# A group norm's root by Ln and Exp and decay differences by Relu on ScalarE, in a state-space layer that TensorE fills

## The chip, the core and the metric

The kernel runs on one core of a Trainium2 chip. A core has TensorE (PE in the profile: matmuls, with PEld for the weight loads), VectorE (DVE), ScalarE (ACT), GpSimd (POOL) and SyncE (SP), each with its own queue of instructions that runs in order; semaphores hold an instruction until what it needs from another engine or a transfer is there. The metric is the device time of one execution in microseconds (us).

## The reference, cut to what matters

Two layers, each a token mixer and a gated FFN, for 512 tokens of width 1024 in float32. Layer 0 mixes by a short convolution, layer 1 by a Mamba-2 state-space layer with 8 groups of 4 heads. Only parts of the second layer are touched:

```python
    cs = jnp.cumsum((dt * a).reshape(bsz, nc, l, g, r), axis=2)
    seg = cs[:, :, :, None] - cs[:, :, None]
    decay = jnp.exp(jnp.where(causal, seg, -jnp.inf)).astype(dtype)
    cb = jnp.einsum('bclgn,bcsgn->bclsg', cm, bm)
    y_diag = jnp.einsum('bclsgr,bcsgrp->bclgrp', cb[..., None] * decay, xdt)
...
    y = y.reshape(bsz, s, M_D_INNER) * jax.nn.silu(z)
    y = rms_normalize(y.reshape(bsz, s, g, M_D_INNER // g)).reshape(bsz, s, M_D_INNER) * norm_g
    return y @ w_out
...
        y = swiglu_ffn(h, f_w_in[i], f_w_out[i])
        x = x + gate * rmsnorm(y, norm_g[i, 3])
```

`rms_normalize` multiplies by `1 / sqrt(mean(x * x) + 1e-6)`.

## The kernel before

Every float32 matrix product is made of three matmuls: an operand is split into a high part (a cast on ScalarE, `act.copy`) and a low part (the rest, a subtraction on VectorE), and high x high, high x low and low x high are summed. Weights come in through the buffer `wst`, their two parts stand in tiles named `whl` or `whlo`, four buffers in a ring.

**The state-space layer** works its eight groups in turn. In all that the code calls `with tc.manual_schedule(...)`, the order in which instructions are written is the order on each engine. While group `cur` is evaluated, the projections of the next one (`nxt`) run on TensorE: four blocks of 24 matmuls for x (two), B and C, two for the gate z. Each of the four goes through `conv4` (L1360): a first step on ScalarE (`act.activation` with Identity, L1363), three on VectorE (L1366), a Silu on ScalarE (L1368). The work of `cur`:

- `prev.root()` and `prev.norm()` finish the group before: `ssg` holds the sums of squares in PSUM, ScalarE takes the root (L1551), VectorE the reciprocal over 128x512 (L1555), and two operations scale the group's outputs `yg` (L1558).
- `e_sub` (L1478): tile `csb` holds, in each of four 512 wide rows, the running sums of one head's decay; from each 128 wide piece a column of `cs_tok` is subtracted and the result clipped at zero from above. Sixteen instructions a group. `e_exp` (L1484): Exp over it, two instructions. `e_mul` (L1489): times the masked products of B and C.
- `step_a`: transposes of x and B and the products of B and C on TensorE, five operations on VectorE (L1433 to L1447), one eviction on ScalarE (`btok`, L1441).
- `states`: matmuls `st` (L1462), then `prev`, the state at the start of each chunk: a copy on ScalarE (L1465) and four small operations on VectorE (L1467, L1469).
- `step_cc`: matmuls `yo` (L1501, they read `prev`) and `yd` (L1512, they read `csb`), then four operations each on VectorE (L1517 to L1520) and the squares on ScalarE. `split_sq` and `sums` split these and sum them over partitions by a matmul (L1547), which gives the next `root` its `ssg`.

The steps of a group on VectorE stand in this order: the scaling of the group before, conv step of x0, a low weight part, `step_a`, `e_mul`, conv step of x1, a low weight part, `prev`, conv step of B, a low weight part, the operations on `yo` and `yd`, conv step of C, two low weight parts, the low part of the squares `sqs` and one more low weight part. Groups 1 to 6 are alike; group 0 is written out by hand ahead of the loop, and in group 7 there is no next group: in the place of its projections stand the first matmuls of the output projection (L381; `y_act`, L1568 and L1569, splits their operands `ys`).

**The layer's end.** `BOUNDARY` is a table of steps written by hand; it finishes the output projection, takes the post norm (`rt1`, L449, a Sqrt; then `x`, L456), the next pre norm (`xs`, L475, squares; `rt3`, L485; `xn`, L493, scaling) and transposes the result (`tr`, L502).

ScalarE's functions come in tables. Before an activation whose function the loaded table lacks, the built program has an ACT_TABLE_LOAD.

**The last FFN's second product** runs as 40 parts (`products`), each with its weights (`w_prep(n)`, L1980 and L1981) and its activations (`a_prep(n)`, L1993 and L1994) split some parts ahead. Four PSUM results, A to D, are collected in two token halves. After part n, `behind(n)` holds what becomes possible: squares for the norm (L2209), a product with the row of gates and norm weights `gg` (`gated`, L2219), sums of the results (L2246, which empties result A after part 33, before part 34 starts it anew). `got["11", t]` is one quarter of the result, in a tile c.

Of the kernel before, what the change touches and what calls it, by code (L numbers as in the profile page):

```python
# [10 lines left out]
AF = mybir.ActivationFunctionType  # L11
ALU = mybir.AluOpType
# [19 lines left out]
MUL, ADD, SUB = ALU.mult, ALU.add, ALU.subtract  # L32
# [6 lines left out]
def trunk_kernel(  # L39
# [9 lines left out]
    act, dve, pe, pool = nc.scalar, nc.vector, nc.tensor, nc.gpsimd  # L49
# [16 lines left out]
    def t2(name):  # L66
        return tmp.tile([P, T], F32, tag="t2", name=name, bufs=4)
# [10 lines left out]
    eps_t = consts.tile([P, 1], F32, name="eps")  # L78
# [501 lines left out]
    with ExitStack() as ph:  # L580
# [549 lines left out]
        def behind(q):  # L1130

            for t in range(2):
                if q == at["s", per - 1]:
                    held[0, t] = t2("c11")
                    act.copy(held[0, t], bank["A", t])
                elif q == at["s", 4 * per - 1]:
                    held[1, t] = t2("c12")
                    act.copy(held[1, t], bank["D", t])
                elif q == at["s", 5 * per - 1]:
                    dve.tensor_tensor(held[1, t], held[1, t], bank["A", t], SUB)  # L1140
                elif q == at["s", 6 * per - 1]:
                    held[1, 2 + t] = c22[:, t, :]
                    act.activation(c22[:, t, :], bank["A", t], AF.Copy, scale=-1.0)
            for p in range(n_s):
                if q == 5 + p // 2:
                    add_(b_("b22", p), b_("b12", p))
                if q == 12 + p:
                    add_(b_("b21", p), b_("b22", p))
                if q == 9 + p:
                    dve.tensor_tensor(b_("b11", p), b_("b22", p), b_("b11", p), SUB)  # L1150

        with tc.manual_schedule(engines={PE_ENGINE, mybir.EngineType.SP, mybir.EngineType.Activation,
# [74 lines left out]
            for q, item in enumerate(seq):  # L1227
                if item[0] == "s":
                    product(item)
                else:  # L1230
                    w = w_of[item]
                    plain_tiles(item[1], [(item[2] + kk, w, kk) for kk in range(2)], item[3])
                behind(q)
                if q in (0, 5):
                    list(rows_g[q // 5])
# [38 lines left out]
    with ExitStack() as ph:  # L1274
# [9 lines left out]
        cs_tok = consts.tile([P, NH, NCH], F32, name="cs_tok")  # L1284
# [89 lines left out]
        class Group:  # L1374
# [96 lines left out]
            def e_sub(self, q):  # L1471

                e = self.e[:, 2 * q:2 * q + 2]
                for hh in range(2):
                    for cc in range(NCH):
                        sl = slice(cc * P, (cc + 1) * P)
                        hd = 4 * self.g + 2 * q + hh
                        dve.tensor_scalar(e[:, hh, sl], e[:, hh, sl], cs_tok[:, hd, cc:cc + 1], 0.0,  # L1478
                                          SUB, ALU.min)

            def e_exp(self, q):

                e = self.e[:, 2 * q:2 * q + 2]
                act.activation(e, e, AF.Exp)  # L1484

            def e_mul(self, q):

# [60 lines left out]

            def root(self):
                self.rg = t2("rg")  # L1550
                act.activation(self.rg, self.ssg, AF.Sqrt, bias=eps_t, scale=1.0 / 256)  # L1551

            def norm(self):
                g = self.g
                dve.reciprocal(self.rg, self.rg)  # L1555
                for q in range(2):
                    y = ygs[2 * g + q]
                    dve.scalar_tensor_tensor(y, y, mng[:, 2 * g + q:2 * g + q + 1], self.rg, MUL, MUL)  # L1558
# [209 lines left out]
    with ExitStack() as ph:  # L1768
# [249 lines left out]
        with tc.manual_schedule(engines={PE_ENGINE, mybir.EngineType.SP, mybir.EngineType.Activation,  # L2018
# [5 lines left out]
            def t3(p):  # L2024
                i = unit_of[p]
                q = units[i].index(p)
                dve.tensor_tensor(b_(i, "b11", q), b_(i, "b22", q), b_(i, "b11", q), SUB)

            def t2_(i):
                add_(b_(i, "b22"), b_(i, "b12"))  # L2030

            def t4(i):
                add_(b_(i, "b21"), b_(i, "b22"))
# [172 lines left out]
            got = {}  # L2206

            def square(t, part, src):
                act.activation(spare["junk"], src, AF.Square, accum_out=st[t]["s2"][:, part:part + 1])  # L2209

            def mean(t):
                dve.tensor_scalar(st[t]["b1"], st[t]["s2"][:, 0:1], 1.0 / D, EPS, MUL, ADD)
# [5 lines left out]
            def gated(src, hf, dst):  # L2218
                dve.tensor_mul(dst, src, gg[hf])  # L2219
                return dst  # L2220

            def x_new(t, hf, yg, parts=(FULL,), puts=(dma,)):
                for c, put in zip(parts, puts):
                    cx = slice(hf * T + c.start, hf * T + c.stop)
                    dve.scalar_tensor_tensor(xt[t][:, cx], yg[:, c], st[t]["s1"], xt[t][:, cx], MUL, ADD)
                    put(out[0, t * P:(t + 1) * P, cx], xt[t][:, cx])

            def behind(n):

                for t in range(2):  # L2230
                    if n == 5:
                        got["11", t] = t2("c11")
                        act.copy(got["11", t], bank["A"][t])
                    elif n == 10:
                        dve.tensor_add(got["11", t], got["11", t], bank["B"][t])
                    elif n == 16:
                        got["12", t] = t2("c12")
                        act.copy(got["12", t], bank["C"][t])
                    elif n == 21:
                        dve.tensor_add(got["12", t], got["12", t], bank["D"][t])  # L2240
                        got["22", t] = spare[f"c22_{t}"]
                        act.copy(got["22", t], bank["D"][t])
                    elif n == 27:
                        dve.tensor_tensor(got["12", t], got["12", t], bank["A"][t], SUB)
                    elif n == 33:
                        dve.tensor_tensor(got["22", t], got["22", t], bank["A"][t], SUB)  # L2246
                    elif n in (29, 30):
                        if t == n - 29:
                            square(t, 0, got["11", t])
                            square(t, 1, got["12", t])  # L2250
                            mean(t)
                    elif n == 31:
                        gated(got["11", t], 0, got["11", t])
                    elif n == 34:
                        root(t)
                    elif n == 35:
                        square(2 + t, 0, got["22", t])
                        mean(2 + t)
                        gated(got["12", t], 1, got["12", t])
                        x_new(t, 0, got["11", t])  # L2260
                    elif n == 36:
                        gated(got["22", t], 1, got["22", t])
                        x_new(t, 1, got["12", t])
                for i, u in enumerate(units):
                    if n == 8 + u[-1] // 2:
                        t2_(i)
                    if n == 19 + i:
                        t4(i)
                for p in {26: (), 27: (), 28: (NP - 2,), 29: (NP - 1,)}.get(n, (n - 17,)):
                    if 0 <= p < NP:  # L2270
                        t3(turns[5][p])

            for n in range(NT - 3):
                if n not in (27, 33):
                    products([n])
                if n in (26, 32):
                    behind(n)
                    products([n + 1])
                    behind(n + 1)
                elif n < 34 and n not in (27, 33):  # L2280
                    behind(n)
                if n == 26:
                    for hf in range(2):
                        dma(gg[hf], gate_d[3, 4 * hf:4 * hf + 4].rearrange("j p -> (j p)").partition_broadcast(P))
                if n + 4 < NT:
                    w_prep(n + 4)
                if n + 3 < NT:
                    a_prep(n + 3)
                if n >= 34:
                    behind(n)  # L2290
            products(range(NT - 3, NT))
            for t in range(2):
                square(2 + t, 1, bank["A"][t])
                yg = gated(bank["A"][t], 0, t2("yg"))
                root(2 + t)
                if t == 0:
                    x_new(2, 0, yg)
                    x_new(2, 1, got["22", 0])
                else:
                    x_new(3, 1, got["22", 1])  # L2300
                    x_new(3, 0, yg, HALVES, (dma_s, dma))
# [29 lines left out]
```

## Time and profile before

| | us |
|---|---|
| median of three runs | 1328.46 (1328.2 to 1328.67) |
| profiled execution, its time | 1328.93 |
| profiled execution, its span | 1327.1 |
| a steady group of the state-space layer | 40.0 |
| TensorE busy | 1313.8 |
| VectorE busy | 1028.0 |
| ScalarE busy | 641.5 |

The span goes from the first to the last instruction, and the execution's own time holds a little more around it. The granted clock of TensorE was 0.999 of full speed on average. The profile gives a source line (L1551) for each instruction, its start and length, and in brackets how long its engine stood idle before it and what ended that. Instructions of one engine overlap a little, so that starts may follow each other more closely than the lengths say.

### The profile page before, as it was taken

How to read it: one execution, taken by the hardware profiler on the slowest of the kernel's cores; microseconds unless marked ns; L12 is line 12 of the kernel's file. 1: busy time of each engine (PE TensorE's matmuls, PEld its weight loads, DVE VectorE, ACT ScalarE, POOL GpSimd, SP SyncE). 2: the span in 40 equal slices, each digit the busy share in tenths (PEclk: the TensorE clock that was granted, in tenths of full speed). 3: DMA queues.
4: the chain of work that ended last, by engine and by line, in shares of the span. 5: the costliest groups of instructions: out<-in, count | busy, mean ns of one | idle time of the engine just before them, and what ended most of it. 6: DMA issues, size and time to landing. Idle time of an engine off the chain costs nothing.

```text
span 1327.1 us, 19226 instructions
## 1 busy us (share of the span) xinstructions
PE 1313.8 (99%) x7437; PEld 1134.4 (85%) x7437; DVE 1028.0 (77%) x1654; ACT 641.5 (48%) x1042; POOL 85.9 (6%) x106
## 2 busy tenths in 40 slices
PE   8999999999999999999999999999999999999997
PEld 7788889888888888898888888888789999998886
DVE  5588866788776686769998989888678777766897
ACT  5322357222222465665554555554574555544665
POOL 0000000000000140000000000000000111101320
PEclk9999999999999999999999999999999999999999
DMA  9757760688885692414534243413252788878961
GB/s 312 230 191 226 247 228 1 214 267 259 286 292 195 178 180 65 130 34 147 159 111 134 74 143 112 143 64 127 85 154 53 190 216 209 200 194 287 177 119 64
DMA packets 203456, 222.21 MB, mean 167 GB/s; under 512 B 8788, under 2 KB 148964, under 8 KB 202340
## 3 DMA queue, kind: packets, MB, share of 16 engines
q1 hardware_dynamic: 186496, 184.74, 44.7%
q0 software_dynamic: 12720, 23.34, 10.2%
q10 hardware_dynamic: 4148, 12.90, 3.0%
q8 instruction: 58, 0.95, 0.3%
q14 instruction: 34, 0.28, 0.1%
HBM read 195.37 MB, written 2.24 MB: 149 GB/s over the span
## 4 chain that ended last, share of the span: by engine, by line
PE 93%; DMA 2%; SPq 2%; DVE 1%; ACT 1%; issue 1%; DVEq 0%; ACTq 0%
PE ip L279 15%; PE ip L281 14%; PE ip L280 14%; PE y L381 8%; PE sA L1920 7%; PE cA L2015 4%; PE cA L1127 3%; PE sC L1920 3%; PE li L279 3%; PE li L281 3%; PE li L280 3%; PE sB L1920 2%; PE li L767 1%; PE yd L1512 1%; PE cC L2015 1%; PE cD L2015 1%
## 5 line engine op out<-in xcount | busy, mean ns | idle before, releaser
L279 PE MATMUL ip<-h,whl 128*128 128x512 f32 x840 | 331.6, 395 | 0.2 <-DVE cv L874 0.2
L281 PE MATMUL ip<-h,whl 128*128 128x512 f32 x840 | 327.6, 390 | 0.0
L280 PE MATMUL ip<-h,whl 128*128 128x512 f32 x840 | 327.4, 390 | 0.0
L279 PEld LDWEIGHTS ip<-h,whl 128*128 128x128 f32 x840 | 157.8, 188 | 33.7 <-issue 1.8
L281 PEld LDWEIGHTS ip<-h,whl 128*128 128x128 f32 x840 | 157.7, 188 | 33.2
L280 PEld LDWEIGHTS ip<-h,whl 128*128 128x128 f32 x840 | 157.9, 188 | 31.7
L225 DVE TENSOR_TENSOR whl<-wst,whl 128x1024 fp32r<-128x1024 f32 x99 | 120.4, 1221 | 41.6 <-ACT whl L224 41.5
L224 ACT CAST whl<-wst 128x1024 fp32r<-128x1024 f32 x99 | 102.3, 1042 | 61.2 <-DMA wst<-in_f_w_in_dram 49.9
L127 DVE SCALAR_TENSOR_TENSOR ada_acc<-ada_st,csil,ada_acc 128x512 f32<-128x512 f32 x140 | 105.0, 750 | 21.5 <-DMA ada_st<-in_ada_w_dram 18.1
L381 PE MATMUL y<-whlo,ys 128*128 128x512 f32 x384 | 89.4, 392 | 0.0
L381 PEld LDWEIGHTS y<-whlo,ys 128*128 128x128 f32 x384 | 71.8, 188 | 15.8 <-issue 0.7
L279 PE MATMUL li<-h,whl 128*128 128x256 f32 x288 | 83.4, 290 | 0.0
L281 PE MATMUL li<-h,whl 128*128 128x256 f32 x288 | 81.7, 284 | 0.0
L280 PE MATMUL li<-h,whl 128*128 128x256 f32 x288 | 81.6, 283 | 0.0
L1920 PE MATMUL sA<-tq,whl 128*128 128x256 f32 x576 | 74.6, 284 | 0.3 <-DVE g L1946 0.3
L1920 PEld LDWEIGHTS sA<-tq,whl 128*128 128x128 f32 x576 | 71.6, 192 | 0.6 <-DVE g L1946 0.5
L1366 DVE SCALAR_TENSOR_TENSOR cu<-ip,cols,cu 128x511 f32<-128x511 f32 (+2 forms) x84 | 62.8, 747 | 4.0 <-ACT cu L1363 1.4
L2015 PE MATMUL cA<-whlo,ao 128*128 128x512 f32 x264 | 61.0, 391 | 1.2 <-ACT whlo L1980 1.0
L2015 PEld LDWEIGHTS cA<-whlo,ao 128*128 128x128 f32 x264 | 49.3, 188 | 12.3 <-ACT whlo L1980 2.0
L1876 DVE TENSOR_TENSOR whl<-wsu,whl 128x1024 fp32r<-128x1024 f32 x33 | 40.4, 1223 | 23.4 <-ACT whl L1875 23.4
L279 PEld LDWEIGHTS li<-h,whl 128*128 128x128 f32 x288 | 55.3, 192 | 0.0
L280 PEld LDWEIGHTS li<-h,whl 128*128 128x128 f32 x288 | 55.3, 192 | 0.0
(371 smaller groups left out, 2319.5 us busy)
## 6 DMA issues: line engine op xcount, KB each, us to landing
ada_st<-in_ada_w_dram SPq DMA_DIRECT2D x96, 512.0 KB, 5.9
wst<-in_f_w_in_dram SPq DMA_DIRECT2D x26, 1024.0 KB, 7.2
wst<-in_m_w_in_dram SPq DMA_DIRECT2D x14, 1024.0 KB, 5.4
wst<-in_m_w_in_dram SPq DMA_DIRECT2D x20, 512.0 KB, 6.0
wst<-in_a_w_in_dram SPq DMA_DIRECT2D x9, 1024.0 KB, 6.8
wsu<-in_f_w_in_dram SPq DMA_DIRECT2D x17, 512.0 KB, 5.5
csb<-cs_d ACTq DMA_DIRECT2D x8, 1024.0 KB, 6.5
sg<-in_f_w_in_dram SPq DMA_DIRECT2D x32, 256.0 KB, 3.4
```

The lines of the kernel that those rows point to most:

```text
L127: dve.scalar_tensor_tensor(acc, w, csil[:, k:k + 1], acc, MUL, ADD)
L224: later.append((lambda sw=sw, w=w: act.copy(w[:, 0, :nk, :], sw), lambda sw=sw, w=w: dve.tensor_tensor(w[:, 1, :nk, :], sw, w[:, 0, :nk, : ...
L225: lambda sw=sw, w=w: dve.tensor_tensor(w[:, 1, :nk, :], sw, w[:, 0, :nk, :].bitcast(F32), SUB)))
L279: pe.matmul(dst, w_at(w, 0, kk), a[:, 0, sl], start=start, stop=False)
L280: pe.matmul(dst, w_at(w, 0, kk), a[:, 1, sl], start=False, stop=False)
L281: pe.matmul(dst, w_at(w, 1, kk), a[:, 0, sl], start=False, stop=stop)
L381: pe.matmul(pst, a[:, al, tk], wt[:, wl, kk, :], start=k == 0 and i == 0, stop=k == K - 1 and i == 2, skip_group_check=bool(held))
L1127: pe.matmul(bank[r, sub], a[:, al, q, tk], w[:, wl, q, :], start=first and k == 0, stop=False, skip_group_check=True)
L1366: dve.scalar_tensor_tensor(u[:, sft:], pst[:, :T - sft], w[3 - sft], u[:, sft:], MUL, ADD)
L1876: dve.tensor_tensor(dst[:, 1], src, dst[:, 0].bitcast(F32), SUB)
L1920: pe.matmul(dst, w[:, wl, k0 + k, :], moving(q, k, al), skip_group_check=True, start=q in ("P1", "P5", "P2") and k == 0 and i == 0, stop=k ...
L2015: pe.matmul(bank[r][sub], a[:, al, q, tk], w[:, hl, q, :], start=first and k == 0, stop=last and k == 2, skip_group_check=True)
```

## The change

Three edits. `root` takes Ln and then Exp with the scale -0.5, which gives the reciprocal root at once, and `norm` loses its reciprocal on VectorE. `e_sub` becomes a Relu on ScalarE, of the column less the piece, and `e_exp` takes the negative of it; VectorE loses sixteen instructions in each group, ScalarE gains as many. In the last FFN `behind` makes the two products of `got["11", t]` with the gates after part 30 and not after part 31.

```diff
-                        dve.tensor_scalar(e[:, hh, sl], e[:, hh, sl], cs_tok[:, hd, cc:cc + 1], 0.0,
-                                          SUB, ALU.min)
+                        act.activation(e[:, hh, sl], e[:, hh, sl], AF.Relu, bias=cs_tok[:, hd, cc:cc + 1],
+                                       scale=-1.0)
...
-                act.activation(e, e, AF.Exp)
+                act.activation(e, e, AF.Exp, scale=-1.0)
...
-                act.activation(self.rg, self.ssg, AF.Sqrt, bias=eps_t, scale=1.0 / 256)
+                act.activation(self.rg, self.ssg, AF.Ln, bias=eps_t, scale=1.0 / 256)
+                act.activation(self.rg, self.rg, AF.Exp, scale=-0.5)
...
-                dve.reciprocal(self.rg, self.rg)
...
                             mean(t)
-                    elif n == 31:
-                        gated(got["11", t], 0, got["11", t])
+                        if n == 30:
+                            gated(got["11", t], 0, got["11", t])
```

On ScalarE, at the start of each of the groups 1 to 6, with the norm's root (`rg`), the weight cast (`whl`), the decays (`csb`) and the first convolution step (`cu`):

```order
 L1551 ACT_TABLE_LOAD
 L1551 ACTIVATE rg<-ssg,eps 128x512
-L224 CAST whl<-wst 128x1024
-L1484 ACT_TABLE_LOAD
+L1552 ACT_TABLE_LOAD
+L1552 ACTIVATE rg<-rg 128x512
+L1478 ACTIVATE csb<-csb,cs_tok 128x128 x16
+L224 CAST whl<-wst 128x1024
 L1484 ACTIVATE csb<-csb 128x1024 x2
 L1363 ACTIVATE cu<-ip,cols_92,cols_93 128x512
```

The norm's Exp and sixteen Relu now stand ahead of the convolution's first step; the second table load moved from the decays' Exp to the norm's.

On ScalarE at the layer's end, where the post norm takes its first Sqrt (`ss`, the sums of squares):

```order
 L206 CAST whl_8223<-wst 128x512
 L433 ACTIVATE xn,ss<-y_7963 128x512
+L449 ACT_TABLE_LOAD
 L449 ACTIVATE ss<-ss 128x1
 L433 ACTIVATE xn,ss<-y_7603 128x512
```

One table load is new there; one more is new at the last group's norm, where Exp follows Ln.

On VectorE in the last FFN, parts 29 to 31 (`whlo` and `ao`: low parts of weights and activations; `c_11179` and `c_11181`: the two halves of `got["11", t]`; `ss`: the norm's first sum):

```order
 L1981 TENSOR_TENSOR whlo<-w2h_10998,whlo 128x512
 L1994 TENSOR_TENSOR ao<-raw,ao 128x512
+L2219 TENSOR_TENSOR c_11179<-c_11179,w2h_10992 128x512
 L2212 TENSOR_SCALAR ss<-ss 128x1
+L2219 TENSOR_TENSOR c_11181<-c_11181,w2h_10992 128x512
 L1981 TENSOR_TENSOR whlo<-w2t_10818,whlo 128x1024
 L1994 TENSOR_TENSOR ao<-raw,ao 128x256
-L2219 TENSOR_TENSOR c_11179<-c_11179,w2h_10992 128x512
-L2219 TENSOR_TENSOR c_11181<-c_11181,w2h_10992 128x512
 L1981 TENSOR_TENSOR whlo<-w2t_10913,whlo 128x1024
```

The two products move ahead of two low parts. TensorE's order is the same in both kernels.

## The prediction

> **What bounds the kernel now.** I read the page first, then the busy time of each engine over one group of the state-space layer, then TensorE's waits.
>
> ```profile
> span 1327.1 us, 19226 instructions
> PE 1313.8 (99%) x7437; PEld 1134.4 (85%) x7437; DVE 1028.0 (77%) x1654; ACT 641.5 (48%) x1042; POOL 85.9 (6%) x106
> 696.36:736.37 40.01, 40.01 (x217) 33.74 (x216) 35.71 (x58) 21.21 (x27) 1.30 (x1) 1.00 0.39 119
> PE cA L2015 <- ACT whlo L1980: 1.0, 1, 1.0
> PE cA L2015 <- DVE c L2244: 0.2, 1, 0.2
> ```
>
> TensorE (PE) is busy for 1313.8 of 1327.1 us. In a group of the state-space layer (third row: PE, weight loads, DVE, ACT) it is busy for all 40.01 us, VectorE for 35.71, ScalarE for 21.21. Nobody makes TensorE wait in that stage, so relieving VectorE can't shorten it. The question is what ScalarE's new work delays, and whether the slack in front of TensorE covers that.
>
> **The steady groups (1 to 6).** ScalarE at the start of such a group, then VectorE behind it, then TensorE's use of the result (the timeline: start, length):
>
> ```profile
> 726.77 1.28 ACT L1551 ACT_TABLE_LOAD   x1 [1.10 <-issue]
> 728.06 0.69 ACT L1551 ACTIVATE rg<-ssg,eps 128x512 f32<-128x512 f32 x1
> ...
> 729.71 1.28 ACT L1484 ACT_TABLE_LOAD   x1
> 731.00 2.01 ACT L1484 ACTIVATE csb<-csb 128x1024 f32<-128x1024 f32 x2
> 732.91 0.76 ACT L1363 ACTIVATE cu<-ip,cols,cols 128x512 f32<-128x512 f32 x1
> ...
> 728.78 3.35 DVE L1555 RECIPROCAL rg<-rg 128x512 f32<-128x512 f32 x1 [1.81 <-ACT rg L1551]
> 733.71 2.32 DVE L1366 SCALAR_TENSOR_TENSOR cu<-ip,cols,cu 128x511 f32<-128x511 f32 x3
> ...
> 747.06 0.42 DVE L1469 TENSOR_TENSOR prev<-prev,st 128x256 f32<-128x256 f32 x1
> ...
> 750.54 1.50 PE L1501 MATMUL yo<-ct,prev 128*128 128x128 f32 x12
> ```
>
> The convolution's first step on ScalarE (L1363) ends at 733.67, and VectorE's part (L1366) starts 0.04 us later. From there VectorE works without a gap, through the low weight parts, step_a, e_mul and the second convolution, to the last `prev` at 747.48 (747.06 + 0.42), 13.77 us on. The first `yo` product that reads it is the third of the first half, some 0.45 us after 750.54 (twelve records in 1.50 us, two for each product): 750.98. The cover is 3.5 us, 3.45 with the 0.04 of a signal.
>
> Ahead of that L1363 ScalarE gets an Exp over 128x512 and sixteen Relu over 128x128. The two table loads (Ln for Sqrt, Exp for Exp) stay two; the second only stands before the norm's Exp now. Ln over the same input is taken at Sqrt's 0.69. The trace has no Relu of this shape with a bias from a column; the nearest rows:
>
> ```profile
> 600.53 0.31 ACT L1335 ACTIVATE dte_tok<-dte_tok 128x128 f32<-128x128 f32 x1 [2.48 <-DVE dte_tok L1334]
> 600.75 0.26 ACT L1336 ACTIVATE dec<-cumT 128x128 f32<-128x128 f32 x1
> ...
> L475 ACT ACTIVATE xn<-x 128x512 f32<-128x512 f32 x21 | 13.1, 626 | 5.0 <-DVE x L456 5.0
> L493 ACT ACTIVATE xn<-x,ss 128x512 f32<-128x512 f32 x12 | 8.0, 712 | 0.1
> ```
>
> A 128x128 activation takes 0.31, and the next starts 0.22 after it (0.09 overlaps). One operand from a column makes a 128x512 one 0.09 longer (712 against 626 ns). So a Relu costs from 0.22 (the column hidden) to 0.40 (no overlap); I take 0.30, the 0.22 plus the 0.09 rounded down. The Exp costs 0.63 less 0.09, 0.53. The shift of L1363 is 0.53 + 16 x 0.30 = 5.33 us, and with it that of `prev`; less the cover of 3.45 it leaves TensorE waiting 1.9 us at `yo`. VectorE is free then: its subtractions and the 3.35 us reciprocal are gone, so nothing else holds L1366. Six groups: **+11.4**. Bounds: at 0.22 the shift is 4.05 and the wait 0.6 (+3.6 in all), at 0.40 it is 6.93 and 3.5 (+21).
>
> Does the delay carry on to the group's next meeting point, the sum of squares?
>
> ```profile
> 711.39 0.56 DVE L1517 TENSOR_TENSOR y<-yo,ecsb 128x384 f32<-128x384 f32 x1 [0.49 <-PE yo L1501]
> 713.10 0.75 DVE L1518 SCALAR_TENSOR_TENSOR yg<-xs,dcol,yd 128x512 f32<-128x512 f32 x1 [1.15 <-PE yd L1512]
> ...
> 722.02 0.68 DVE L1538 TENSOR_TENSOR sqs<-accg,sqs 128x512 fp32r<-128x512 f32 x1
> 724.87 0.62 PE L1547 MATMUL ssg<-sqs,ones_r 128*128 128x512 f32 x2
> ```
>
> Against TensorE, which itself has moved by 1.9, VectorE comes out of `prev` 3.45 us late. It used to wait 0.49 + 1.15 = 1.64 us in the rest of the group and makes those up, so `sqs` is 1.8 us late against a cover of 2.17 (724.87 less 722.70). It just holds, by 0.4, and the next group starts in step.
>
> In group 0 the first eight Relu fall ahead of an instruction that waited 2.75 us for TensorE, the other eight and the Exps ahead of an e_mul that VectorE reached at 623.71:
>
> ```profile
> 616.43 0.78 ACT L1363 ACTIVATE cu<-ip,cols,cols 128x512 f32<-128x512 f32 x1 [2.75 <-PE ip L281]
> 623.71 2.35 DVE L1489 TENSOR_TENSOR csb<-csb,cbm 128x1024 f32<-128x1024 f32 x2
> ```
>
> Eight Relu are 2.4 us, and VectorE no longer subtracts there: nothing.
>
> **Group 7** has no convolutions; ScalarE's next work there are weight and operand splits for the output projection.
>
> ```profile
> 889.39 2.20 ACT L1484 ACTIVATE csb<-csb 128x1024 f32<-128x1024 f32 x2
> 891.49 1.98 ACT L206 CAST whlo<-wsto 128x1024 fp32r<-128x1024 f32 x2
> 893.38 0.61 ACT L1568 CAST ys<-yg 128x512 fp32r<-128x512 f32 x1
> ...
> 895.12 2.35 DVE L207 TENSOR_TENSOR whlo<-wsto,whlo 128x1024 fp32r<-128x1024 f32 x2
> 897.39 0.69 DVE L1569 TENSOR_TENSOR ys<-yg,ys 128x512 fp32r<-128x512 f32 x1
> 900.71 1.89 DVE L1569 TENSOR_TENSOR ys<-yg,ys 128x512 fp32r<-128x512 f32 x3
> ...
> 898.27 7.10 PE L381 MATMUL y<-whlo,ys 128*128 128x512 f32 x30
> ```
>
> The same 5.33 moves the first weight cast to 896.8 (it ends near 897.85), `ys` to 898.7. VectorE starts the two low parts at 897.9, is through at 900.2 (2.27, from 895.12 to 897.39) and ends the low `ys` at 900.9. TensorE's third matmul of the block (30 in 7.10 us, 0.23 each: 898.27 + 0.45 = 898.7) needs it: 2.2 late. The next operand's low part comes after step_a (2.7 us, to 900.71 in the row), at 904.2, where TensorE by then wants it at 903.6: another 0.6. **+2.8** (1.4 at the low price, 4.3 at the high one).
>
> **The layer's end.** Before, Sqrt's table stayed loaded from the last norm to the post norm at L449. Now the last norm ends in Exp, and L449 loads Sqrt again.
>
> ```profile
> 971.80 0.29 ACT L449 ACTIVATE ss<-ss 128x1 f32<-128x1 f32 x1
> ...
> 973.64 0.63 ACT L475 ACTIVATE xn<-x 128x512 f32<-128x512 f32 x1 [0.98 <-DVE x L456]
> 978.24 1.32 ACT L493 ACTIVATE xn<-x,ss 128x512 f32<-128x512 f32 x2
> ...
> 979.47 0.70 PE L502 MATMUL xtr<-ident,xn 128*128 128x128 f32 x4
> ```
>
> L475 waits for an x that follows from L449, and from there ScalarE works in one row to L493, which ends at 979.56; the transposes that read it start at 979.47 and take 0.70. There is no cover, so of the load's 1.28 us (row 729.71) **+1.2** shows. The last norm itself (Ln, load, Exp instead of Sqrt and the 3.35 us reciprocal) gets shorter, off the path. The Trainium skill, "ScalarE: Activation LUTs", section "What ACT_TABLE_LOAD costs", adds a drain of about 1.38 us to each load's 1.28; by it this term would be an estimated 2.6 and the sum 1.4 higher. Here the trace disagrees: the load at 729.71 ends at 730.99 and Exp starts at 731.00.
>
> **The last FFN.** Two products by the gate row (L2219) leave a place shortly ahead of TensorE's one longer wait for one where VectorE stood idle:
>
> ```profile
> 1301.17 1.29 DVE L2219 TENSOR_TENSOR c<-c,w2h 128x512 f32<-128x512 f32 x2
> ...
> 1304.11 1.28 DVE L2246 TENSOR_TENSOR w2h<-w2h,cA 128x512 f32<-128x512 f32 x2
> ...
> 1304.94 15.30 PE L2015 MATMUL cA<-whlo,ao 128*128 128x512 f32 x66 [0.99 <-ACT whlo L1980]
> ```
>
> The wait is put down to a weight cast, but the first of the two L2246 empties the very bank (A) that TensorE's next product starts, and ends at 1304.75. With L2219 out of its way VectorE reaches it about 1.2 us sooner, and the first half of that bank is finished before the second: the wait goes, **-0.95** (0 if the cast is the cause). The end of the kernel follows TensorE, so this shows in full.
>
> **Sum:** 11.4 + 2.8 + 1.2 - 0.95 = +14.5. The profiled execution took 1328.93 (its span 1327.1 and 1.8 around it), 0.47 above the median of the runs, 1328.46; against the median this is 1343.0.
>
> **Rivals.** (1) ScalarE's small activations run at 0.22: 3.6 + 1.4 + 1.2 - 0.95 = +5.3, 1333.7. For it stands only that the column's 0.09 was seen on larger tiles. (2) One load fewer: if Ln and Exp were served by one table, the second load of each group would go, the shift be 5.33 - 1.28 = 4.05, and the time again 1333.7. Against it stands the built order, with a load before each. The Trainium skill, same page, section "Table sets: the hidden batching unit", has such a set and counts one load for Ln followed by Exp; by that rule this rival would hold, and before's trace, with no Ln, can't show it. (3) A second wait: the 0.4 us left at `sqs` fails, or Relu doesn't overlap. At 0.40 the sum is 21 + 4.3 + 1.2 - 0.95 = +25.6, 1354; half a microsecond a group at `sqs` gives 1346. (4) Faster: TensorE's modelled busy time hides pauses for VectorE in the groups, and taking off its 3.35 us reciprocal and sixteen subtractions shortens them. With ScalarE's shift covered, 0.5 us a group in six groups and the FFN's 0.95 give 1324.5; it decides once VectorE, not TensorE, is late at `yo`. The rows say the reverse: VectorE waited for `yo` and `yd`. (5) The cover at `yo` suffices, as it would at 0.18 a Relu: only the end of the layer and the FFN show, +0.3, 1328.8.
>
> **Chances:** forecast 0.68, (1) 0.09, (2) 0.04, (3) 0.12, (4) 0.02, (5) 0.05. A measurement of this kernel can tell about 0.2%, 2.7 us, from no change: faster 0.02, same 0.05, slower 0.93. The range is 1334 to 1352: from just above the low price to most of the way to the high one.
>
> **What would show it.** In the changed trace: sixteen Relu at 0.30 each in a row; L1366 some 5.3 us later against the group's start; groups of 41.9 instead of 40.0 us, with TensorE waiting at L1501 for VectorE's `prev` and not at L1547; a wait of 2 to 3 us at L381 in group 7; a table load at L449 and a wait of 1.2 at L502; the 0.99 at L2015 gone. Groups still of 40.0 us would make the prediction wrong.

## The result: 1.15% slower, and the profile after

The changed kernel takes 1343.5 us (median of four runs, 1343.13 to 1345.47) against 1328.39 before (also four): the ratio is 1.0115, with an interval of 1.0102 to 1.0128. Of the page after, the span and the busy times, and then what TensorE waited for, longest first (total, times, longest):

```profile
span 1341.7 us, 19223 instructions
PE 1318.1 (98%) x7437; PEld 1135.2 (85%) x7437; DVE 976.9 (73%) x1518; ACT 684.1 (51%) x1180; POOL 85.9 (6%) x106
PE yo L1501 <- DVE prev L1469: 8.1, 12, 0.9
...
PE y L381 <- DVE ys L1569: 1.9, 3, 0.8
...
PE y L381 <- ACT ys L1568: 0.6, 1, 0.6
PE xtr L502 <- ACT xn L493: 0.5, 2, 0.3
...
PE cA L2015 <- DVE w2h L2246: 0.2, 1, 0.2
```

VectorE works 51 us less than before, ScalarE 43 more, and TensorE has a wait that before's list did not have: `yo` for the last two `prev`, twelve times, two in each of the groups 1 to 6. One such group after: ScalarE, VectorE and TensorE (start, length).

```profile
730.39 1.28 ACT L1551 ACT_TABLE_LOAD   x1 [1.13 <-issue]
731.68 0.69 ACT L1551 ACTIVATE rg<-ssg,eps 128x512 f32<-128x512 f32 x1
732.39 1.28 ACT L1552 ACT_TABLE_LOAD   x1
733.68 0.63 ACT L1552 ACTIVATE rg<-rg 128x512 f32<-128x512 f32 x1
734.22 4.78 ACT L1478 ACTIVATE csb<-csb,cs_tok 128x128 f32<-128x128 f32 x16
738.91 1.04 ACT L224 CAST whl<-wst 128x1024 fp32r<-128x1024 f32 x1
739.85 2.00 ACT L1484 ACTIVATE csb<-csb 128x1024 f32<-128x1024 f32 x2
741.75 0.76 ACT L1363 ACTIVATE cu<-ip,cols,cols 128x512 f32<-128x512 f32 x1
...
742.54 2.32 DVE L1366 SCALAR_TENSOR_TENSOR cu<-ip,cols,cu 128x511 f32<-128x511 f32 x3 [6.78 <-ACT cu L1363]
...
755.89 0.42 DVE L1469 TENSOR_TENSOR prev<-prev,st 128x256 f32<-128x256 f32 x1
...
754.13 0.38 PE L1501 MATMUL yo<-ct,prev 128*128 128x128 f32 x2
755.38 0.49 PE L1501 MATMUL yo<-ct,prev 128*128 128x128 f32 x2 [0.87 <-DVE prev L1469]
756.37 1.16 PE L1501 MATMUL yo<-ct,prev 128*128 128x128 f32 x8 [0.49 <-DVE prev L1469]
```

From the first table load to L1363 it is 11.36 us (741.75 less 730.39); before it was 6.14. VectorE stands idle for 6.78 us waiting for that one instruction, the longest idle time in its group, and `yo`, which before ran in one piece, now waits 0.87 and 0.49. The list of waits holds only part of the loss, 8.1 us for `yo` where the six groups grew by 11.3: broken into three pieces the products themselves also count longer. From their first start to their last end they take 3.40 us here (754.13 to 757.53) against 1.50 before, and that is the 1.9 by which the group grew.

To see where the 14.6 us of span went, I cut the span at TensorE's first instructions: the first and the last sum of squares (`ssg`, groups 1 to 6 lie between them), the transposes of group 7 (`xtok`), the last group's sum of squares, the last FFN's first product into `sA` (L1920), and the end. Lengths in us, worked out from the starts in each trace, one profiled execution for each kernel; the kernels e1 to e9 are the experiments below:

| | groups 1 to 6 | first output block | group 7 | layer's end | last FFN to end |
|---|---|---|---|---|---|
| before | 240.08 | 11.34 | 34.33 | 99.29 | 297.26 |
| after | 251.42 | 12.69 | 36.88 | 99.67 | 296.42 |
| after less before | +11.34 | +1.35 | +2.55 | +0.38 | -0.84 |
| forecast | +11.4 | 0 | +2.8 | +1.2 | -0.95 |
| e1, Relu alone | +8.55 | +1.36 | +2.03 | -0.09 | -0.09 |
| e2, root alone | 0.00 | 0.00 | -0.02 | +0.61 | -0.08 |
| e3, FFN alone | 0.00 | 0.00 | 0.00 | -0.11 | -0.82 |
| e4, eight Relu | 0.00 | +0.87 | +0.35 | +0.10 | -0.87 |
| e9, twelve Relu | +4.64 | +1.36 | +1.38 | +0.98 | -0.83 |
| e5, conv step first | 0.00 | -0.01 | +2.51 | +0.04 | -0.85 |
| e6, and group 7 | 0.00 | 0.00 | -0.02 | -0.08 | -0.83 |
| e7, early Sqrt | +11.46 | +1.35 | +2.58 | -0.14 | -0.84 |
| e8, e6 and e7 | 0.00 | 0.00 | -0.02 | +0.15 | -0.84 |

The five differences of the changed kernel sum to 14.78; the -0.19 that leads to 14.6 lies ahead of the first cut.

### The profile page after: what moved, and what is told of

It is laid out like the page before. It is cut to its first block, busy times and chain, and to the rows that moved or that the text cites. A ratio compares the mean times of both kernels' runs of the same rounds, so it can differ in the third digit from the quotient of the medians.

```text
span 1341.7 us, 19223 instructions
## 1 busy us (share of the span) xinstructions
PE 1318.1 (98%) x7437; PEld 1135.2 (85%) x7437; DVE 976.9 (73%) x1518; ACT 684.1 (51%) x1180; POOL 85.9 (6%) x106
## 4 chain that ended last, share of the span: by engine, by line
PE 75%; DVE 10%; ACT 9%; issue 2%; SPq 2%; DMA 2%; ACTq 1%; DVEq 0%
PE ip L279 10%; PE ip L281 10%; PE ip L280 10%; PE y L381 7%; PE sA L1920 6%; PE cA L2015 4%; PE cA L1127 3%; PE sC L1920 3%; ACT csb L1478 2%; DVE cu L1366 2%; PE li L279 2%; PE li L281 2%; PE li L280 2%; PE sB L1920 2%; DVE whl L225 1%
## 5 line engine op out<-in xcount | busy, mean ns | idle before, releaser
L1366 DVE SCALAR_TENSOR_TENSOR cu<-ip,cols,cu 128x511 f32<-128x511 f32 (+2 forms) x84 | 62.8, 747 | 44.0 <-ACT cu L1363 42.0
L1920 PE MATMUL sA<-tq,whl 128*128 128x256 f32 x576 | 74.6, 283 | 0.3 <-DVE g L1946 0.3
L1920 PEld LDWEIGHTS sA<-tq,whl 128*128 128x128 f32 x576 | 71.6, 192 | 0.6 <-DVE g L1946 0.5
```

The source lines that it names most:

```text
L1366: dve.scalar_tensor_tensor(u[:, sft:], pst[:, :T - sft], w[3 - sft], u[:, sft:], MUL, ADD)
L1920: pe.matmul(dst, w[:, wl, k0 + k, :], moving(q, k, al), skip_group_check=True, start=q in ("P1", "P5", "P2") and k == 0 and i == 0, stop=k ...
```

## The experiments

**Each edit alone.** e1 has the Relu edit, e2 the root's, e3 the FFN's, as in the change's diff.

> Only the Relu edit; the norm's root and the FFN as before. Theory (the sixteen Relu ahead of L1363 run into prev and yo): the shift is 4.8 us instead of 5.33, each of the groups 1 to 6 grows by 1.35 us (8.1 in all), the first output block ahead of group 7 waits 1.35 as in the changed kernel, group 7 itself about 2.0, nothing at the layer's end: +11.5, 1339.9 us. Rival (Ln, Exp and their table loads carry the loss): under half of the changed kernel's 15 us, below 1336.

1340.51 us, ratio 1.009 (1.0076 to 1.0103). Groups grow by 1.43 us each, the first output block by 1.36, group 7 by 2.03: the Relu edit alone brings four fifths of the loss, and the rival is out.

> Only the norm's root by Ln and Exp. Theory: ScalarE's chain moves by 0.53 us, inside the cover of 3.45 at yo and of 0.6 in group 7, so groups stay at 40.0 us; only the Sqrt load at L449 shows, 0.4 us as the changed kernel's trace has it: 1328.8 us. The prediction's own step would give 1.2: 1329.6. Rival (the root's loads carry the loss): 7 us or more, 1335.

1329.04 us, ratio 1.0002 (0.9993 to 1.0011). The groups are those of before to the hundredth; all that shows is 0.6 at the layer's end. The time can't tell 0.4 from 1.2 there; the stage speaks against 1.2, though its length also varies with a transfer, as shown below. On top of the Relu the root does cost the groups something: the changed kernel's grow by 0.46 more than e1's (1.89 less 1.43), near its Exp's own 0.54. The same 0.54 is free while there is cover left and paid when the Relu have used it up.

> Only the two gated products one part sooner. Theory (VectorE reaches L2246, which empties bank A, late): the wait of 0.99 us at L2015 shrinks to about 0.2, -0.8: 1327.6 us. Rival (the weight cast named by the profile is the cause): no change, 1328.4.

1327.79 us, ratio 0.9995 (0.9986 to 1.0003): the times alone don't separate it from before. The stage does: 0.82 less in the last FFN, and the same in all kernels with the edit. TensorE's wait before part 34 in e3:

```profile
1303.80 2.55 PE L2015 MATMUL cA<-whlo,ao 128*128 128x512 f32 x10 [0.19 <-DVE w2h L2246]
```

The 0.99 before, put down to a weight cast on ScalarE, is 0.19 now and put down to L2246, although ScalarE has the same instructions in the same order. The cast that the profile named, before and in e3:

```profile
1304.20 0.61 ACT L1980 CAST whlo<-w2s 128x512 fp32r<-128x512 f32 x1
...
1303.85 0.61 ACT L1980 CAST whlo<-w2s 128x512 fp32r<-128x512 f32 x1
```

Before, it ended 0.02 us behind the first L2246 (both near 1304.8), and the product started at 1304.94. In e3 it ends at 1304.46, 0.66 us after the product has started. So TensorE doesn't need the cast for this product; VectorE held the bank.

**How much Relu.** e4 leaves eight of a group's sixteen on ScalarE:

```diff
+                        if q == 0:
                             act.activation(e[:, hh, sl], e[:, hh, sl], AF.Relu, bias=cs_tok[:, hd, cc:cc + 1],
                                            scale=-1.0)
+                        else:
+                            dve.tensor_scalar(e[:, hh, sl], e[:, hh, sl], cs_tok[:, hd, cc:cc + 1], 0.0,
+                                              SUB, ALU.min)
...
-                act.activation(e, e, AF.Exp, scale=-1.0)
+                act.activation(e, e, AF.Exp, scale=-1.0 if q == 0 else 1.0)
```

> The changed kernel with eight of the sixteen clipped differences of a group back on VectorE (the first pair of heads by Relu, the second as before). Theory (a cover of 3.45 us, a threshold): the shift is 0.53 + 8 x 0.30 = 2.93, under the cover, so groups stay at 40.0 us; VectorE is still 2.9 - 1.6 = 1.3 us late at the end of group 6, where the first output block has 0.3 of cover: +1.0; layer's end +0.4, FFN -0.8: 1329.0 us. Rival (each Relu costs TensorE its share, without a threshold): about half of the loss, 1336.

1329.42 us, ratio 1.0006 (0.9997 to 1.0015). None of the groups 1 to 6 grows: `prev` is done 0.6 us ahead of its reader (750.04 against 750.66 in one of them). The lateness that is left at the end of group 6 shows in the first output block (from the timeline of TensorE, the start of that block):

```profile
884.61 0.62 PE L1551 MATMUL ssg<-sqs,ones_r 128*128 128x512 f32 x2
885.06 0.61 PE L381 MATMUL y<-whlo,ys 128*128 128x512 f32 x2
886.25 1.42 PE L381 MATMUL y<-whlo,ys 128*128 128x512 f32 x5 [0.58 <-DVE ys L1573]
```

The block is 0.87 longer where 1.0 was expected; group 7 is 0.35 longer, which the expectation left out. e9 has twelve: the last head's four are made by the subtraction and a multiplication by -1 on VectorE.

```diff
+                        if q == 0 or hh == 0:
                             act.activation(e[:, hh, sl], e[:, hh, sl], AF.Relu, bias=cs_tok[:, hd, cc:cc + 1],
                                            scale=-1.0)
+                        else:
+                            dve.tensor_scalar(e[:, hh, sl], e[:, hh, sl], cs_tok[:, hd, cc:cc + 1], 0.0,
+                                              SUB, ALU.min)
+                            dve.tensor_scalar(e[:, hh, sl], e[:, hh, sl], -1.0, None, MUL)
```

> The changed kernel with twelve of the sixteen clipped differences of a group by Relu (the last head's four by two instructions each on VectorE, in a stretch where it stood idle). Theory (a threshold, then one for one): the shift is 0.53 + 12 x 0.30 = 4.1 us, 0.7 over the cover, so groups of 40.7 us (4.2 in six), 1.35 at the first output block, about 1.4 in group 7, layer's end 0.0 to 0.7, FFN -0.8: 1335.1 us. Rival (the loss is in proportion to the number of Relu, from 1329.4 at eight to 1343.5 at sixteen): 1336.5, and groups of 41.0 us.

1336.21 us, ratio 1.0053 (1.0036 to 1.0069). The time lies nearer to the rival's; the stages tell why, and speak for the threshold. Groups grow by 0.77 us on average, from 0.66 to 1.00 (0.7 and 1.0 were expected), the first output block by 1.36 and group 7 by 1.38, as the theory had them; the rest is the layer's end, at 0.98 its longest here. Zero at eight Relu, 0.77 a group at twelve, 1.89 at sixteen: nothing up to the cover, and beyond it, by the 1.12 for the last four Relu, 0.28 for each, close to the Relu's own 0.30.

**The same work in another order.** e5 moves one line of the changed kernel's loop; e6 also moves three in group 7:

```diff
                 prev.root()
+                next(conv2[0])
                 for q in range(2):
                     cur.e_sub(q)
...
                 prev.norm()
                 next(conv2[0])
-                next(conv2[0])
...
             prev.root()
+            ops = next(parts[0])
+            for op in ops[:3]:
+                op()
             for q in range(2):
                 cur.e_sub(q)
             for q in range(2):
                 cur.e_exp(q)
             prev.norm()
-            ops = next(parts[0])
-            for op in ops[:3]:
-                op()
             cur.step_a()
```

> The changed kernel with the convolution's first step (L1363 of x0) put ahead of the sixteen Relu in groups 1 to 6; the same instructions otherwise. Theory (order on ScalarE, not the amount of its work): L1366 starts as early as before, the next low weight part some 1.4 us late, under the cover; groups of 40.0 us and no wait at the first output block; group 7 still +2.6, layer's end +0.4, FFN -0.8: 1330.6 us. Rival (ScalarE's added 4.8 us a group cost by their amount): no gain, 1343.

1330.45 us, ratio 1.0015 (1.0006 to 1.0024). ScalarE in a group of e5, and VectorE's `prev`:

```profile
730.73 0.78 ACT L1363 ACTIVATE cu<-ip,cols,cols 128x512 f32<-128x512 f32 x1 [0.24 <-PE ip L281]
731.41 4.78 ACT L1478 ACTIVATE csb<-csb,cs_tok 128x128 f32<-128x128 f32 x16
...
748.35 0.42 DVE L1469 TENSOR_TENSOR prev<-prev,st 128x256 f32<-128x256 f32 x1
```

L1363 now goes as soon as its projection is finished, and the sixteen Relu stand behind it at their full 4.78 us. `prev` is done at 748.77, before its reader starts at 750.75. Groups are at 40.0 us again and the first output block loses nothing: 13 of the 15 us were an order, not an amount.

> e5, and in group 7 the two weight splits and the first operand split ahead of the Relu. Theory: group 7's waits at L381 go too; layer's end +0.4 and FFN -0.8 remain: 1328.0 us. Rival (group 7 loses by something else, e.g. the operand ring): 1330 or more.

1328.05 us, ratio 0.9997 (0.9988 to 1.0006): group 7 is at before's length, so what it lost was the weight and operand splits queued behind the Relu.

**The load at the layer's end.** e7 is the changed kernel with one more line, e8 is e6 with it:

```diff
             cur.root()
+            act.activation(small(1), eps_t, AF.Sqrt)
             cur.norm()
```

> The changed kernel with one dummy Sqrt over 128x1 right behind the last norm's Exp, so that Sqrt's table is loaded there and not at L449. Theory: the 0.4 us between the first and the second group of transposes at the layer's end go: 1343.1 us. The prediction's step (the whole load shows): 1342.3. Rival (the 0.4 has another cause): 1343.5.

1343.11 us, ratio 1.0112 (1.0098 to 1.0126): as expected from the 0.4, though a run against e7's own range (1342.91 to 1344.31) doesn't settle 0.4. Nor does the stage alone: 99.67 becomes 99.15 here, but in e8, with the same dummy Sqrt, it is 99.44 against e6's 99.21 without. What the load costs is read from a piece of the stage, below under the layer's end.

> e6 with the dummy Sqrt of e7: all of the change, with each of its delays under cover. Theory: only the FFN's gain is left, 1327.6 us, the same as e3, although VectorE does 6.6 us less in each group; nothing of its relief reaches TensorE. Rival (relief of VectorE is worth something once ScalarE is no longer in the way): below 1326.5.

1327.71 us, ratio 0.9995 (0.9986 to 1.0004), and e3's 1327.79. A group of e8 by engines (PE, weight loads, DVE, ACT, POOL), the answer to the row of before at the head of the prediction:

```profile
695.71:735.73 40.02, 40.02 (x217) 33.74 (x216) 29.06 (x40) 26.31 (x45) 1.30 (x1) 1.00 0.39 119
```

VectorE has 29.06 us of work where it had 35.71, every delay is covered, and the group still takes 40.02. The relief is worth nothing there. e3 and e8 are the fastest kernels here; the runs can't tell them from before or from each other, and only their last FFN, in the trace, is shorter.

## Why the prediction was right, and where it was not

**The steady groups** went by its steps. Sixteen Relu take 4.78 us (0.30 each, one 0.39 alone: the column's 0.09 and the overlap of 0.09 hold for the small tile); the root's Exp adds 0.54 (733.68 to 734.22); VectorE's chain from L1366 to `prev` is 13.77 us, unchanged (742.54 to 756.31). Against the group's sum of squares L1366 comes 5.23 us later (742.54 less 728.47, 733.71 less 724.87); less the 1.89 that the group grew, the cover was 3.34, a tenth below the 3.45 read off, as the shift is a tenth below 5.33. Six groups lost 11.34 where 11.4 was forecast, and none, eight, twelve and sixteen Relu show the cover as a threshold. The rivals are out: (1) the Relu is not at 0.22, (2) both loads are there (732.39), (3) the Relu overlap and `sqs` stays in time in these groups, (4) relief shortens nothing, (5) the cover does not suffice.

**Where the lateness went next** was missed. The prediction followed VectorE to `sqs` and found 0.4 us of cover. A group after, then the first output block before and after:

```profile
768.97 0.69 DVE L1538 TENSOR_TENSOR sqs<-accg,sqs 128x512 fp32r<-128x512 f32 x1
770.37 0.61 PE L1547 MATMUL ssg<-sqs,ones_r 128*128 128x512 f32 x2
...
884.86 2.49 DVE L1569 TENSOR_TENSOR ys<-yg,ys 128x512 fp32r<-128x512 f32 x4
...
885.38 11.04 PE L381 MATMUL y<-whlo,ys 128*128 128x512 f32 x48
...
897.46 2.50 DVE L1569 TENSOR_TENSOR ys<-yg,ys 128x512 fp32r<-128x512 f32 x4
...
896.67 0.73 PE L381 MATMUL y<-whlo,ys 128*128 128x512 f32 x2
898.20 10.72 PE L381 MATMUL y<-whlo,ys 128*128 128x512 f32 x46 [0.80 <-DVE ys L1569]
```

In the groups that held, with 0.7 left (769.66 against 770.37). But the group after the sixth starts with the output projection, whose operand parts stand behind `sqs` in VectorE's queue; the text ahead of the prediction calls the groups 1 to 6 alike, and at the end of group 6, which has these splits in place of the next group's low weight parts, they are not. Before, the first of the low parts was done at 885.55 and wanted at 885.8, with 0.3 us of cover. Now it ends 2.08 us after the start of the block's sum of squares (898.15 against 896.07) where it took 0.63, so it is 1.45 later, and TensorE waits. The prediction's own 1.8 of lateness at `sqs`, less this 0.3, would have given 1.5. The step that failed is "the next group starts in step": it is not so for the last one, +1.35. In e5, where `prev` is in time, the block is back at 11.33.

**Group 7**: 2.55 against 2.8, along the steps given:

```profile
910.98 0.61 ACT L1568 CAST ys<-yg 128x512 fp32r<-128x512 f32 x1
...
912.44 0.68 DVE L1569 TENSOR_TENSOR ys<-yg,ys 128x512 fp32r<-128x512 f32 x1
...
911.64 0.73 PE L381 MATMUL y<-whlo,ys 128*128 128x512 f32 x2 [0.63 <-ACT ys L1568]
913.18 3.00 PE L381 MATMUL y<-whlo,ys 128*128 128x512 f32 x12 [0.80 <-DVE ys L1569]
916.50 8.00 PE L381 MATMUL y<-whlo,ys 128*128 128x512 f32 x34 [0.32 <-DVE ys L1569]
```

The high part of the operand, its low part, and the next operand's low part: three waits in one place. Against the start of the group's transposes the block's third matmul comes 1.9 us later than before, where 2.2 was forecast, and the fifteenth, which takes the next operand's low part, another 0.6, as forecast.

**The layer's end** was mis-sized: 0.38 against 1.2. VectorE there before, then the changed kernel:

```profile
969.65 2.50 DVE L207 TENSOR_TENSOR whl<-wst,whl 128x512 fp32r<-128x512 f32 x4
972.06 0.69 DVE L439 TENSOR_TENSOR yg<-y,gg 128x512 f32<-128x512 f32 x1
972.66 0.16 DVE L452 RECIPROCAL ss<-ss 128x1 f32<-128x1 f32 x1
...
983.67 2.18 ACT L206 CAST whl<-wst 128x512 fp32r<-128x512 f32 x4 [0.83 <-DMA wst<-in_f_w_in_dram]
...
986.46 1.28 ACT L449 ACT_TABLE_LOAD   x1
987.75 0.29 ACT L449 ACTIVATE ss<-ss 128x1 f32<-128x1 f32 x1
...
988.08 0.16 DVE L452 RECIPROCAL ss<-ss 128x1 f32<-128x1 f32 x1 [0.66 <-ACT ss L449]
...
995.04 0.55 PE L502 MATMUL xtr<-ident,xn 128*128 128x128 f32 x3 [0.27 <-ACT xn L493]
```

"There is no cover" was wrong on one count: before, the reciprocal at L452 did not start when L449 ended (972.09) but 0.57 us later, since VectorE was still at low weight parts and the product behind them; now it waits 0.66 for L449. From the start of the four casts (983.67) to the end of L493 (994.99) it is 11.32 us in the changed kernel and 11.31 or 11.32 in the five experiments with this load, 10.56 to 10.60 in before and the four without: the load costs 0.75 of its 1.28, and that is the term's size. The rest is where the four casts start, which is set by a weight transfer (the 0.83): 38.41 us after the last sum of squares before, 38.03 after, and from 37.57 to 38.62 in all. Behind L493 the stage takes another 50.3 us, in all kernels but e3 and e7. So the 0.38 is the load's 0.75 less a start about 0.37 earlier, and with the load the stage lost from nothing to 0.98. In e7 too the casts start earlier than in the changed kernel, by 0.27, and behind L493 it takes 0.5 us more (50.8), so its 0.52 is not the load's cost alone. What sets the landing wasn't tried.

**The last FFN**: 0.84 against 0.95. The bank was the cause, as e3 shows; 0.19 us stays, the end of the first L2246:

```profile
1318.69 1.37 DVE L2246 TENSOR_TENSOR w2h<-w2h,cA 128x512 f32<-128x512 f32 x2 [0.33 <-PE cA L2015]
1319.53 15.30 PE L2015 MATMUL cA<-whlo,ao 128*128 128x512 f32 x66 [0.19 <-DVE w2h L2246]
```

Together, +1.35 missed, and 0.8 too much at the layer's end and 0.25 in group 7: 1343.0 against 1343.5 is as close as that by luck. The groups were forecast by the mechanism that the runs show; of the rest, errors in opposite directions nearly cancel, and half of the one at the layer's end is a transfer that landed early.

## What to carry to other kernels

An engine that is half idle is not free at every point of its queue: before moving work to it, look up what stands behind the new place, how late that may be, and follow the lateness to every later meeting with the bounding engine, the ones after the loop too. Where such a move costs, try the order first: one line put ahead of the new work gave back 11 of 15 us in the loop, and the waits behind it. And relief for an engine that the bounding one never waits for is worth nothing, here 6.65 us of 35.71 in each group.

## What the runs showed of the hardware

A wait's name in the profile was wrong by a small margin: the 0.99 us before part 34 went to a cast that ended 0.02 us behind L2246, and only taking work off VectorE showed which it was. The table load at 732.39 took 1.28 us and no more: it starts 0.02 after Ln ends (731.68 + 0.69), and Exp starts at 733.68, 0.01 after it. The load at L449 cost 0.75 of its 1.28 on the path, because VectorE's work beside it had held the reciprocal back before.
